# Two more pairs of the up-projection through Strassen's scheme, their mixed inputs summed on ScalarE and VectorE

## The chip, the cores and the metric

The kernel runs on one core of a Trainium2 chip. The metric is the device time of one launch in microseconds. Before the change three timed runs gave 702.15, 702.4 and 703.0 us, with a median of 702.4 us. Engines are named as the profile names them: PE is TensorE, PEld its weight loads, DVE is VectorE, ACT is ScalarE, POOL is GpSimd, and SP is SyncE, which here only issues transfers.

## The reference

One decoder layer on 512 tokens with a width of 1024: a combined input projection, two causal attentions of 8 heads each (block-sparse and stick-breaking), gates, an output projection and a residual, then a gated convolution block. The change lies in that last block:

```python
h = rms_norm(x, g_ffn[layer])
u = causal_depthwise_conv(h @ w_up[layer], conv_w[layer], conv_b[layer])   # h: 512 x 1024, w_up: 1024 x 5632
u_gate, u_val = jnp.split(u, 2, axis=-1)                                   # 2816 columns each
x = x + (jax.nn.silu(u_gate) * u_val) @ w_down[layer]
```

Everything is float32.

## The kernel before

**Three products for one.** A float32 operand is split into a high and a low part, each in the type that TensorE multiplies: ACT copies the high part (`hi`, `whi`), DVE subtracts it from the original to get the low part (`lo`, `wlo`). `mm3` (lines 90 to 92) then issues three matmuls: high by high, high by low, low by high.

**Pairs.** The up-projection is cut into 22 pairs. Pair i is a tile of 128 gate columns and the matching tile of 128 value columns; its contraction over 1024 runs in eight blocks of 128. `h2` holds the normalized input, transposed and split, for all eight blocks. A plain pair (`plain`, `up_mm`) is 2 columns tiles x 8 blocks x 3 = 48 matmuls that stream 512 tokens each. Its weights are two tiles of 128x1024, each split on the way by ACT (line 85) and DVE (line 86). The first two pairs are done in eight halves of 256 tokens (`up_half`), since the second half of the tokens is ready earlier; their weight tiles are the four entries of `wup`.

**Mixed pairs.** Pairs 4 to 19 (`MIXED`) go through the Winograd form of Strassen's scheme. Gate and value, the two halves of the tokens and the two halves of the contraction make a 2x2 by 2x2 block product, which takes seven block products of 256 tokens: 7 x 4 blocks x 3 = 84 matmuls. `first_four(i)` issues four of the seven, called X, Q, Y and Z here after the quarters of PSUM that they fill, `last_three(i)` the other three; the loop issues `first_four` of the next pair before `last_three` of the last one. X and Q use plain rows of `h2`; Y and Z of `first_four` and the first and last of `last_three` use four sums of quarters of the input, held split in `tm4` (tiles `xa7` to `xa10`).

**Weights of a mixed pair.** Four tiles: `wa` straight from the weights, `wb` and `wc` sums of weight quarters, `wd` a half tile straight from the weights. The sums (`usum`) are made in DRAM by accumulating transfers on POOL's queue, 16 pairs one after another, while the attention runs. The low part of `wc` is made ahead, too: during the gate stage `split_ahead` fetches the sum (`praw`), ACT writes its high part into a spare PSUM tile (line 604), DVE subtracts, and POOL stores the result (`ulo`); `last_three` later fetches it from there by SP straight into the `wlo` slot (line 991). ACT (line 992) and DVE (line 994) split everything else. High and low parts stand in rings of three slots each (`wsp`), so a weight tile can be written when the matmuls of the one three places before it have finished.

**Mixed inputs.** `h32` (tiles `xa5`, `xa6`) is the input in float32: 16 transfers on POOL's queue copy the high parts and accumulate the low parts (lines 1031 and 1033) behind pairs 0 and 1, while PE works on plain pairs 2 and 3. `mixes` makes the four sums on DVE and splits each (lines 965 to 971).

**Order.** PE runs in program order, by hand. The other engines' orders come from a scheduler; each engine takes its queue in order. Behind the products of a pair stand, on ACT and DVE, the sums of its seven parts (lines 1007 to 1024) and `glu` (lines 911 to 928, then 576 to 579 and 337/338): convolution, gate, and the sums for the down-projection. These free the PSUM banks: eight banks, two per pair.

## Time and profile before

| what | value |
| --- | --- |
| median of three timed runs | 702.4 us (702.15 to 703.0) |
| the profiled execution's own time | 701.36 us |
| its span | 699.6 us |
| PE busy | 690.9 us (99%), 4460 matmuls seen |
| PEld busy | 604.3 us (86%) |
| DVE busy | 573.7 us (82%) |
| ACT busy | 404.3 us (58%) |
| POOL busy | 123.8 us (18%) |
| plain pairs 2 and 3 on PE | 391.20 to 412.98 us |
| mixed pairs 4 to 19 on PE | 412.98 to 565.31 us |

Times inside the span are microseconds from its start. A row of the timeline gives the start, the duration, the engine, the line, the operation, output and inputs, the shape and the count; in brackets stands how long the engine had been idle before it and what ended that. The profile's page gives matmuls a duration of 0.28 or 0.39 us, but they overlap in a pipeline: what a matmul costs is the distance from one start to the next.

### The profile page before, as it was taken

The page shows a single profiled execution, that of the slowest core. Times are in us where ns is not written, and L with a number is a line of the kernel's source. Part 1 is how long each engine was busy: PE and PEld are TensorE (multiplying, and loading weights), DVE is VectorE, ACT ScalarE, POOL GpSimd, SP SyncE. Part 2 cuts the span into 40 slices and gives each one's busy share as a digit, 9 for nine tenths or more (in the row PEclk, how much of TensorE's full clock was granted, in tenths as well). Part 3 has the DMA queues.
Part 4 walks back from the last instruction along what each step waited for, and adds up shares of the span by engine and source line. Part 5 has one row for each costly group of instructions (what it writes and reads, how often), then busy time and mean ns, then how long its engine had stood idle before and what let it go on. Part 6 is the DMA issues. An engine that isn't in the chain of part 4 may idle for free.

```text
span 699.6 us, 11729 instructions
## 1 busy us (share of the span) xinstructions
PE 690.9 (99%) x4460; PEld 604.3 (86%) x4460; DVE 573.7 (82%) x901; ACT 404.3 (58%) x607; POOL 123.8 (18%) x200
## 2 busy tenths in 40 slices
PE   9999999999999999999999999999999999999995
PEld 6888888979888888888889889999999988888884
DVE  7778858598694777586876899989999998878996
ACT  6435445455564455445576666777777764546854
POOL 1211122233542122112312410000000003200000
PEclk9999999999999999999999999999999999999999
DMA  8799999999999688787998968889777765867703
GB/s 313 277 339 368 358 353 238 240 237 246 228 266 291 230 294 273 270 270 273 350 340 290 208 176 300 291 306 326 250 240 250 261 220 199 311 209 249 265 0 121
DMA packets 57577, 184.13 MB, mean 263 GB/s; under 512 B 6640, under 2 KB 7408, under 8 KB 51632
## 3 DMA queue, kind: packets, MB, share of 16 engines
q1 hardware_dynamic: 41136, 105.18, 42.5%
q0 software_dynamic: 16096, 77.87, 39.8%
q8 instruction: 35, 0.57, 0.3%
q10 hardware_dynamic: 288, 0.33, 0.1%
q14 instruction: 22, 0.18, 0.1%
HBM read 162.64 MB, written 64.75 MB: 325 GB/s over the span
## 4 chain that ended last, share of the span: by engine, by line
PE 98%; DVE 1%; ACT 1%; DMA 1%; issue 0%; ACTq 0%
PE b L92 12%; PE b L90 12%; PE b L91 12%; PE mm L90 11%; PE mm L92 11%; PE mm L91 11%; PE c L91 5%; PE c L90 5%; PE c L92 5%; PE q L209 3%; PE tp L480 3%; PE tp L504 3%; PE sc L404 1%; PE sc L414 1%; PE v L91 1%; PE v L90 1%
## 5 line engine op out<-in xcount | busy, mean ns | idle before, releaser
L90 PE MATMUL b<-h,whi 128*128 128x256 f32 (+1 forms) x320 | 95.8, 299 | 0.0
L91 PE MATMUL b<-h,whi 128*128 128x256 f32 (+1 forms) x320 | 95.7, 299 | 0.0
L92 PE MATMUL b<-h,wlo 128*128 128x256 f32 (+1 forms) x320 | 95.7, 299 | 0.0
L90 PE MATMUL mm<-xg,whi 128*128 128x512 f32 x224 | 89.8, 401 | 0.0
L85 ACT ACTIVATE whi<-raw 128x1024 fp32r<-128x1024 f32 (+2 forms) x62 | 59.8, 975 | 51.4 <-PE mm L92 16.8
L92 PE MATMUL mm<-xg,wlo 128*128 128x512 f32 x224 | 87.4, 390 | 0.0
L91 PE MATMUL mm<-xg,whi 128*128 128x512 f32 x224 | 87.3, 390 | 0.0
L992 ACT ACTIVATE whi<-raw 128x1024 fp32r<-128x1024 f32 x64 | 61.1, 954 | 37.5 <-PE b L91 28.1
L86 DVE TENSOR_TENSOR wlo<-raw,whi 128x1024 fp32r<-128x1024 f32 (+2 forms) x62 | 68.6, 1115 | 12.9 <-ACT whi L85 12.6
L90 PE MATMUL b<-xa,whi 128*128 128x256 f32 x256 | 70.7, 276 | 0.0
L91 PE MATMUL b<-xa,whi 128*128 128x256 f32 x256 | 70.7, 276 | 0.0
L672 ACT ACTIVATE whi<-raw 128x1024 fp32r<-128x1024 f32 x45 | 46.8, 1052 | 31.9 <-DVE raw L690 11.8
L90 PEld LDWEIGHTS b<-h,whi 128*128 128x128 f32 x320 | 60.1, 188 | 2.5
L91 PEld LDWEIGHTS b<-h,whi 128*128 128x128 f32 x320 | 60.1, 188 | 2.5
L92 PEld LDWEIGHTS b<-h,wlo 128*128 128x128 f32 x320 | 60.1, 188 | 2.5
L672 DVE TENSOR_TENSOR wlo<-raw,whi 128x1024 fp32r<-128x1024 f32 x45 | 54.7, 1221 | 5.7 <-ACT whi L672 5.6
L92 PE MATMUL b<-xa,wlo 128*128 128x256 f32 x192 | 53.0, 276 | 0.0
L90 PEld LDWEIGHTS mm<-xg,whi 128*128 128x128 f32 x224 | 42.1, 188 | 9.9 <-issue 1.8
L92 PEld LDWEIGHTS mm<-xg,wlo 128*128 128x128 f32 x224 | 42.0, 188 | 9.0
L91 PEld LDWEIGHTS mm<-xg,whi 128*128 128x128 f32 x224 | 42.2, 188 | 7.9
L91 PEld LDWEIGHTS b<-xa,whi 128*128 128x128 f32 x256 | 48.1, 188 | 0.0
L90 PEld LDWEIGHTS b<-xa,whi 128*128 128x128 f32 x256 | 48.1, 188 | 0.0
(282 smaller groups left out, 1747.4 us busy)
## 6 DMA issues: line engine op xcount, KB each, us to landing
raw<-w SPq DMA_DIRECT2D x103, 512.0 KB, 5.8
usum<-w POOLq DMA_DIRECT2D x16, 1024.0 KB, 25.6
raw<-usum SPq DMA_DIRECT2D x32, 512.0 KB, 5.2
usum<-w POOLq DMA_DIRECT2D x16, 512.0 KB, 19.6
usum<-usum POOLq DMA_DIRECT2D x32, 256.0 KB, 12.0
praw<-usum POOLq DMA_DIRECT2D x16, 512.0 KB, 5.6
ulo<-praw POOLq DMA_DIRECT2D x16, 512.0 KB, 5.3
wlo<-ulo SPq DMA_DIRECT2D x32, 256.0 KB, 3.6
```

Source lines behind the costliest of these rows:

```text
L85: wload.hi = nc.scalar.activation(hi[:, sl], raw[:, sl], AF.Copy)
L86: wload.lo = nc.vector.tensor_sub(lo[:, sl], raw[:, sl], hi[:, sl].bitcast(F32))
L90: nc.tensor.matmul(ps, a[0], b[0], start=start, stop=False, **kw)
L91: nc.tensor.matmul(ps, a[0], b[1], start=False, stop=False, **kw)
L92: nc.tensor.matmul(ps, a[1], b[0], start=False, stop=stop, **kw)
L209: nc.tensor.matmul(qk0[c], w0[i][:, (k % 2) * 512 + c * 128:(k % 2) * 512 + (c + 1) * 128], xg[k][:, j], start=(k == 0 and n == 0), stop=( ...
L404: nc.tensor.matmul(scs[h // 2][:, h % 2, o:o + n], Q[i][r0:r0 + 32, c, qt * 128:(qt + 1) * 128], K[i][r0:r0 + 32, d, :n], start=False, sto ...
L414: nc.tensor.matmul(sc[:, h, o:o + n], q[r0:r0 + 64, c, qt * 128:(qt + 1) * 128], k[r0:r0 + 64, d, :n], start=m == 0, stop=m == 2, skip_gro ...
L480: nc.tensor.transpose(tp[:, h, c:c + 128], a[:, h, c:c + 128], ident)
L504: nc.tensor.matmul(av[h * 64:(h + 1) * 64, j, qt * 128:(qt + 1) * 128], v[:, kb, (2 * p + h) * 64:(2 * p + h + 1) * 64], aT[p][:, h, o + k ...
L672: splits.append((nc.scalar.activation(hi, raw, AF.Copy), nc.vector.tensor_sub(lo, raw, hi.bitcast(F32))))
L992: nc.scalar.activation(hi[:, :n], raw[:, :n], AF.Copy)
```

## The change

Pairs 2 and 3 become mixed pairs (`MIXED = range(2, 20)`), so the mixed inputs are wanted right behind the first two pairs, where before two plain pairs stood in between.

- The 16 transfers that made `h32` are gone. ACT reads the first half of the tokens once more from the transposed PSUM banks (line 1054 of the new file, eight instructions of 128x256); DVE adds the high and low parts of the second half (line 1056, two of 128x1024). `mixes` needs one operation per sum as before, in another order, and hands out the four split inputs one by one; the splits of weights of the first mixed pair are put behind them (`early`, `ready`) by a new helper `behind`, which only puts instructions later in their engine's order.
- The last of the `up_half` calls run in the order 2, 0, 1, 3.
- POOL's queue makes the weight sums of 17 pairs (2 to 18) ahead; those of pair 19 are made later, in four steps behind pairs 8, 10, 12 and 14.
- `split_ahead` makes 16 low parts as before, but others: those of `wc` for pairs 2 to 15 and those of `wb` for pairs 2 and 3. Those of `wc` for pairs 16 to 19 are now split in the loop, by DVE.
- The small steps for the down-projection's sums behind pairs 0 to 2 are tied to another tile, and two small copies swap places at the end.

```diff
-MIXED = range(4, 20)
+MIXED = range(2, 20)
-AHEAD = MIXED
+AHEAD = sorted([(i, 1) for i in MIXED[:14]] + [(i, 0) for i in MIXED[:2]], key=lambda q: (q[0], -q[1]))
...
-        sums_of(MIXED)
+        for _ in sums_of(MIXED[:17]):
+            pass
+    lastsums = sums_of(MIXED[17:])
...
-    ulo = {i: wdr.tile([128, 2, 512], F32R, name=f"ulo{i}") for i in AHEAD}
+    ulo = {(i, h): wdr.tile([128, 2, 512], F32R, name=f"ulo{i}{h}") for i, h in AHEAD}
...
-        i = ahead.pop(0)
+        q = i, h = ahead.pop(0)
         raw = psp.tile([128, 2, 512], F32, name="praw", bufs=3)
-        nc.gpsimd.dma_start(raw, both(usum[i][2:4]))
+        nc.gpsimd.dma_start(raw, both(usum[i][2 * h:2 * h + 2]))
...
-    h2 = [x1s.tile([128, 2, S], F32R, name=f"h2{k}") for k in range(KT)]
+    h2all = x1s.tile([128, KT, 2, S], F32R, name="h2")
+    h2 = [h2all[:, k] for k in range(KT)]
...
-    for n in range(4):
+    for n in (2, 0, 1, 3):
         up_half(ups[n], wup[n], 0)
...
-        nc.vector.tensor_sub(b11, b11, b12)
-        nc.vector.tensor_sub(b12, b22, b12)
-        nc.vector.scalar_tensor_tensor(b22, b11, -1.0, b22, op0=OP.mult, op1=OP.subtract)
-        nc.vector.scalar_tensor_tensor(b21, b22, -1.0, b21, op0=OP.mult, op1=OP.subtract)
-        for n, q in enumerate((b11, b22, b12, b21)):
-            nc.scalar.activation(tm4[n][:, 0], q, AF.Copy)
-            nc.vector.tensor_sub(tm4[n][:, 1], q, tm4[n][:, 0].bitcast(F32))
+        def halve(n, q, sign=1.0):
+            hi, lo = tm4[n][:, 0], tm4[n][:, 1]
+            act = nc.scalar.activation(hi, q, AF.Copy, scale=sign)
+            return act.ins, nc.vector.scalar_tensor_tensor(lo, q, sign, hi.bitcast(F32), op0=OP.mult, op1=OP.subtract).ins
+        nc.vector.tensor_sub(b22, b22, b12)
+        yield halve(2, b22)
+        nc.vector.tensor_sub(b12, b11, b12)
+        yield halve(0, b12)
+        nc.vector.tensor_add(b11, b11, b22)
+        yield halve(1, b11, -1.0)
+        nc.vector.tensor_sub(b21, b11, b21)
+        yield halve(3, b21)
...
     def first_four(i):
-        wa = wmix(i, [(slice(0, 1024), w[WIDX["up", i, 0]])])
-        wb = wmix(i, [(None, both(usum[i][0:2]))])
+        with behind(early if i == MIXED[0] else ()):
+            wa = wmix(i, [(slice(0, 1024), w[WIDX["up", i, 0]])])
+            wb = wmix(i, [(None, both(usum[i][0:2]))], lo=ulo.get((i, 0)))
...
     def last_three(i, ps1, ps2, p1s, v):
-        wc = wmix(i, [(None, both(usum[i][2:4]))], lo=ulo.get(i))
+        wc = wmix(i, [(None, both(usum[i][2:4]))], lo=ulo.get((i, 1)))
...
+        if i in range(8, 16, 2):
+            step(lastsums, u[:, 0, :1])
...
-    for i in range(2):
-        plain(i)
-    for k in range(KT):
-        nc.gpsimd.dma_start(h32[k // 4][:, k % 4], h2[k][:, 0].bitcast(F32))
-    for k in range(KT):
-        nc.gpsimd.dma_start(h32[k // 4][:, k % 4], h2[k][:, 1].bitcast(F32), accum_op=OP.add)
-    for i in range(2, MIXED[0]):
-        if i == MIXED[0] - 1:
-            mixes()
-        plain(i)
+    for k in (0, 2, 1, 3, 4, 6, 5, 7):
+        src = turn_banks[0, k // 4][k % 4 // 2][:, k % 2 * 256:(k % 2 + 1) * 256]
+        nc.scalar.activation(h32[k // 4][:, k % 4, :256], src, AF.Copy, scale=gffn[:, k:k + 1])
+    for h in range(2):
+        nc.vector.tensor_add(quad(h, 1), *(h2all[:, 4 * h:4 * h + 4, c, 256:].bitcast(F32) for c in range(2)))
+    mixed_in = mixes()
+    early = next(mixed_in)
+    ready = next(mixed_in)
+    for i in range(MIXED[0]):
+        with behind(next(mixed_in, ())):
+            plain(i)
```

The rows of the program's order that follow name an instruction's line, operation, output and inputs with their buffer numbers, and shape.

**First place: DVE between the transposed input and the first product behind the `up_half` calls.** Before, the eight low parts of `h2` (line 808) are followed by the splits of two plain weight tiles and the convolutions of pairs 0 and 1:

```order
L808 SCALAR_TENSOR_TENSOR h25_3393<-b2_3379,vecs_85,h25_3393 128x256
L808 SCALAR_TENSOR_TENSOR h27_3395<-b3_3380,vecs_85,h27_3395 128x256
L86 TENSOR_TENSOR wlo_4170<-raw_4168,whi_4169 128x1024
L86 TENSOR_TENSOR wlo_4201<-raw_4199,whi_4200 128x1024
L912 SCALAR_TENSOR_TENSOR t0_4119<-b6_3850,vecs_85,t0_4119 128x511
L912 SCALAR_TENSOR_TENSOR t1_4123<-b7_3851,vecs_85,t1_4123 128x511
```

Now the input's float32 sums, the mixes and their low parts stand there, and the split of `wa` of pair 2 (`wlo_4176`) among them:

```order
L815 SCALAR_TENSOR_TENSOR h2_3394<-b3_3386,vecs_85,h2_3394 128x256
L1056 TENSOR_TENSOR xa5_4107<-h2_3394 128x4x256
L1056 TENSOR_TENSOR xa6_4108<-h2_3394 128x4x256
L978 TENSOR_TENSOR xa6_4108<-xa6_4108,xa5_4107 128x4x256
L980 TENSOR_TENSOR xa5_4107<-xa5_4107 128x4x256
L976 SCALAR_TENSOR_TENSOR xa9_4111<-xa6_4108,xa9_4111 128x1024
L982 TENSOR_TENSOR xa5_4107<-xa5_4107,xa6_4108 128x4x256
L1008 TENSOR_TENSOR wlo_4176<-raw_4174,whi_4175 128x1024
L976 SCALAR_TENSOR_TENSOR xa7_4109<-xa5_4107,xa7_4109 128x1024
L984 TENSOR_TENSOR xa6_4108<-xa5_4107,xa6_4108 128x4x256
L976 SCALAR_TENSOR_TENSOR xa8_4110<-xa5_4107,xa8_4110 128x1024
L919 SCALAR_TENSOR_TENSOR t0_4138<-b6_3849,vecs_85,t0_4138 128x511
```

The convolutions of pairs 0 and 1 have moved behind the third of the four mixed inputs.

**Second place: SP's queue there.** Before, only raw weights and sums are loaded until the first `wc`. Now the low parts of `wb` of pairs 2 and 3 (`ulo20`, `ulo30`) and of `wc` of pair 2 (`ulo21`) stand between the loads:

```order
L1002 DMA raw_4306<-usum2_433 128x2x512
L1005 DMA wlo_4182<-ulo20_2627 128x512 x2
L1002 DMA raw_4313<-w 128x512
L1002 DMA raw_4373<-w 128x1024
L1005 DMA wlo_4248<-ulo30_2629 128x512 x2
L1005 DMA wlo_4308<-ulo21_2626 128x512 x2
L1002 DMA raw_4379<-usum4_435 128x2x512
```

Each of the three writes a `wlo` slot and so stands in the queue until the matmuls on the slot's last tile are done.

**Third place: DVE around the last mixed pairs.** Before, between the products of pair 18 and those of pair 19 (`wlo_6261` and `wlo_6267` are `wa` and `wb` of pair 19, `whi_6332` is the half tile `wd` of pair 18; `wc` comes from DRAM):

```order
L338 TENSOR_TENSOR xa1_5986<-tm_5857,xa1_5986 128x1024
L994 TENSOR_TENSOR wlo_6261<-raw_6259,whi_6260 128x1024
L1009 TENSOR_TENSOR xb8_4095<-b1_6137,xb8_4095 128x256
L1022 TENSOR_TENSOR u_6238<-b4_6006,xb9_4096 128x256
L1023 TENSOR_TENSOR u_6238<-b4_6006,xb9_4096 128x256
L928 TENSOR_TENSOR tm_6121<-t0_6112,t1_6116 128x2x256
L994 TENSOR_TENSOR wlo_6267<-raw_6265,whi_6266 128x1024
L1024 TENSOR_TENSOR u_6238<-b5_6007,xb10_4097 128x512
L577 TENSOR_TENSOR tm_6121<-tm_6121 128x256
L994 TENSOR_TENSOR whi_6332<-raw_6331,whi_6332 128x512
```

Now (`wlo_6378` and `wlo_6384` are `wa` and `wb` of pair 19, `wlo_6443` is `wc` of pair 18):

```order
L1008 TENSOR_TENSOR wlo_6378<-raw_6376,whi_6377 128x1024
L585 TENSOR_TENSOR xb7_4093<-tm_5976,xb7_4093 128x256
L1031 TENSOR_TENSOR xb8_4094<-b1_6255,xb8_4094 128x256
L921 SCALAR_TENSOR_TENSOR t1_6234<-u_6226,vecs_85,t1_6234 128x510
L344 TENSOR_TENSOR xa1_6105<-tm_5976,xa1_6105 128x1024
L1008 TENSOR_TENSOR wlo_6384<-raw_6382,whi_6383 128x1024
L1044 TENSOR_TENSOR u_6355<-b4_6125,xb9_4095 128x256
L1045 TENSOR_TENSOR u_6355<-b4_6125,xb9_4095 128x256
L1046 TENSOR_TENSOR u_6355<-b5_6126,xb10_4096 128x512
L1008 TENSOR_TENSOR wlo_6443<-raw_6441,whi_6442 128x1024
L937 TENSOR_TENSOR tm_6239<-t0_6230,t1_6234 128x2x256
L1008 TENSOR_TENSOR whi_6448<-raw_6447,whi_6448 128x512
```

The split of `wc` is new there, and the sums, the convolution and the gate product of earlier pairs have moved behind the splits of weights.

More of the change, by code (lines that the diff above doesn't have):

```diff
@@ L279, in sums_of @@
                     nc.gpsimd.dma_start(usum[i], flat(("ui", i, 0), 2), max_dma_last_dim=8192)
+                yield
                 for i in group:
                     adds(usum[i][0:2], flat(("ui", i, 2), 1))
+                yield
                 for i in group:
                     adds(usum[i][3], usum[i][0])
+                yield
                 for i in group:
                     adds(usum[i][2], usum[i][3])
-        sums_of(MIXED)
+                yield
+        for _ in sums_of(MIXED[:17]):
+            pass
+    lastsums = sums_of(MIXED[17:])
     mqkp = pool(ysta, "mqkp", 4, side="right")
@@ L595, in both, with step @@
         return q.rearrange("h p c -> p h c")
+    dsums = (step for q in dsum.items() for step in quarter_sums("di", [q]))
+    marks = iter(list(range(16, 31)) + list(range(16)))
+    def step(todo, src):
+        c = next(marks, None)
+        if c is None:
+            return
+        seen = small[:, c:c + 1]
+        nc.vector.tensor_copy(seen, src)
+        with tc.issue_after(nc.gpsimd.tensor_copy(seen, seen).ins):
+            next(todo, None)
     def split_ahead():
@@ L607, in split_ahead @@
             nc.vector.tensor_sub(lo, raw, phi.bitcast(F32))
-        nc.gpsimd.dma_start(ulo[i], lo)
+        nc.gpsimd.dma_start(ulo[q], lo)
     for i in range(KT):
@@ L656, in trunk_layer @@
     splits = []
-    dsums = (step for q in dsum.items() for step in quarter_sums("di", [q]))
-    marks = iter(list(range(16, 31)) + list(range(8)))
-    def step(todo, src):
-        c = next(marks, None)
-        if c is None:
-            return
-        seen = small[:, c:c + 1]
-        nc.vector.tensor_copy(seen, src)
-        with tc.issue_after(nc.gpsimd.tensor_copy(seen, seen).ins):
-            next(todo, None)
     def split_in(p, raw):
@@ L927, in glu @@
         j = i // 2
+        if i < 3:
+            step(dsums, uc[0][:, :1])
         split = a_side(i % 2, lambda dst: nc.vector.tensor_mul(dst, ua, ub), glu.tm, xa[j] if i % 2 else None, xb[j])
@@ L939, in glu @@
                     nc.gpsimd.dma_start(away["a", j][:, h], xa[j][:, h])
-        if i < 3:
-            step(dsums, xb[j][:, 0, :1] if i % 2 else glu.tm[:, 0, :1])
         return split
@@ L995, in wmix, with behind @@
         return hi, wlo
+    def behind(ins):
+        st = ExitStack()
+        for q in ins:
+            st.enter_context(tc.issue_after(q))
+        return st
     def first_four(i):
-        wa = wmix(i, [(slice(0, 1024), w[WIDX["up", i, 0]])])
-        wb = wmix(i, [(None, both(usum[i][0:2]))])
+        with behind(early if i == MIXED[0] else ()):
+            wa = wmix(i, [(slice(0, 1024), w[WIDX["up", i, 0]])])
+            wb = wmix(i, [(None, both(usum[i][0:2]))], lo=ulo.get((i, 0)))
         ps1, ps2 = up_ps(), up_ps()
@@ L1006, in first_four @@
         p1s, p5s, v = (tmp[i % 2][:, n] for n in range(3))
-        nc.scalar.activation(p1s, X, AF.Copy)
+        with behind(ready if i == MIXED[0] else ()):
+            nc.scalar.activation(p1s, X, AF.Copy)
         nc.scalar.activation(p5s, Y, AF.Copy)
@@ L1025, in last_three @@
                              ps2.rearrange("p (n c) -> p n c", n=2), u2[:, None].to_broadcast([128, 2, 256]))
+        if i in range(8, 16, 2):
+            step(lastsums, u[:, 0, :1])
         return glu(i, (u[:, 0], u[:, 1]))
-    for i in range(2):
-        plain(i)
-    for k in range(KT):
-        nc.gpsimd.dma_start(h32[k // 4][:, k % 4], h2[k][:, 0].bitcast(F32))
-    for k in range(KT):
-        nc.gpsimd.dma_start(h32[k // 4][:, k % 4], h2[k][:, 1].bitcast(F32), accum_op=OP.add)
-    for i in range(2, MIXED[0]):
-        if i == MIXED[0] - 1:
-            mixes()
-        plain(i)
+    for k in (0, 2, 1, 3, 4, 6, 5, 7):
[9 more added lines that the diff above has]
+            plain(i)
     prev = None
     for i in MIXED:
-        cur = i, *first_four(i)
+        with behind(ready if i == MIXED[0] + 1 else ()):
+            cur = i, *first_four(i)
         if prev:
```

## The prediction

> **What bounds the kernel now.** I read the page first: engines, slices, the chain that ended last.
>
> ```profile
> span 699.6 us, 11729 instructions
> PE 690.9 (99%) x4460; PEld 604.3 (86%) x4460; DVE 573.7 (82%) x901; ACT 404.3 (58%) x607; POOL 123.8 (18%) x200
> PE   9999999999999999999999999999999999999995
> DVE  7778858598694777586876899989999998878996
> PE 98%; DVE 1%; ACT 1%; DMA 1%; issue 0%; ACTq 0%
> ```
>
> PE is busy in every slice but the last and makes up 98% of the chain: matmul time taken away shortens the run one for one, unless PE then waits. DVE is the next engine, at nine tenths and more where the mixed pairs run, so it is where a wait would come from. Then PE's starts at three edges, and the windows between them:
>
> ```profile
> 391.20 0.40 PE L90 MATMUL b<-h,whi 128*128 128x512 f32 x1
> 412.98 0.28 PE L90 MATMUL b<-h,whi 128*128 128x256 f32 x1
> 565.31 0.40 PE L90 MATMUL b<-h,whi 128*128 128x512 f32 x1
> 391.20:412.98 21.78, 21.78 (x98) 18.02 (x97) 19.58 (x30) 12.91 (x15) 6.75 (x10) 1.00 0.93 209
> 412.98:565.31 152.33, 152.33 (x1345) 152.32 (x1344) 144.94 (x226) 112.30 (x169) 4.39 (x8) 1.00 0.79 272
> ```
>
> A window's columns are its length, then the busy time of PE, PEld, DVE, ACT and POOL, the granted clock, the share of DMA and GB/s. Plain pairs 2 and 3 take 21.78 us, the sixteen mixed pairs 152.33 us; PE has no gap in either, at full clock.
>
> **What goes and what comes on PE.** Two plain pairs are 96 matmuls of 512: 21.78 / 96 = 0.227 us each. Sixteen mixed pairs are 16 x 84 = 1344 of 256: 152.33 / 1344 = 0.1133 us, half as much, so a mixed pair costs 152.33 / 16 = 9.52 us. Two of them take 19.04 us, and PE gains 21.78 - 19.04 = **2.74 us**.
>
> The half price has to hold for the added 168 matmuls. The Trainium skill, TensorE: Matmul & The Clock Gate, section Back-to-back issue gap, speaks against it: weight loads and matmuls together set a sustained spacing of about 81 ns at N=128 and 131 ns at N=512. On a straight line through the two a 256-wide matmul would take 98 ns, an estimate from that page, and the change would cost 168 x 98 - 96 x 131 ns = 3.9 us. This trace does not agree: 227 ns and 113 ns. The worst 256-wide spacing in the trace is that of one `up_half`:
>
> ```profile
> 385.60 0.28 PE L90 MATMUL b<-h,whi 128*128 128x256 f32 x1
> 385.72 0.28 PE L91 MATMUL b<-h,whi 128*128 128x256 f32 x1
> ```
>
> At 0.12 us the gain would be 21.78 - 168 x 0.12 = 1.62 us. I take 0.1133, the mean of the 1344 matmuls of the very form that is added.
>
> **The gap in front of pair 2.** The order of PE up to 391.20 keeps its count, so X of pair 2 starts there; by 12 matmuls a quarter (1.36 us), Q starts at 392.6, Y at 393.9, Z at 395.3, pair 3 at 396.6, `last_three(2)` at 402.1 and its last quarter at 404.8. What has to be ready:
>
> ```profile
> 379.08 0.86 ACT L807 ACTIVATE h<-b,vecs 128x256 fp32r<-128x256 f32 x2 [0.21 <-DVE h L808]
> 382.96 1.06 ACT L85 ACTIVATE whi<-raw 128x1024 fp32r<-128x1024 f32 x1 [3.02 <-PE b L91]
> 385.68 1.06 ACT L85 ACTIVATE whi<-raw 128x1024 fp32r<-128x1024 f32 x1 [1.66 <-PE b L91]
> 379.58 0.88 DVE L808 SCALAR_TENSOR_TENSOR h<-b,vecs,h 128x256 fp32r<-128x256 f32 x2 [0.15 <-ACT h L807]
> 410.82 1.22 DVE L966 TENSOR_TENSOR xa<-xa,xa 128x1024 f32<-128x1024 f32 x1
> 411.95 0.74 DVE L914 SCALAR_TENSOR_TENSOR t<-b,vecs,t 128x510 f32<-128x510 f32 x1
> 380.46:384.06 3.60, 3.60 (x34) 3.60 (x33) 0.01 (x2) 1.06 (x1) 2.50 (x4) 1.00 1.01 390
> ```
>
> `h2` is done at 379.94 on ACT and 380.46 on DVE, and behind it DVE stood idle for 3.6 us. A DVE operation of 128x1024 takes 1.13 us to the next start (410.82 to 411.95), an ACT read of 128x256 0.42 (half of 0.86), an ACT split 1.06. No row shows line 1056's sum of strided parts; it moves as much as L966 and is taken as that, 1.13, with 2 x 1.13 as the upper bound. The scale and sign of the other forms change no shape.
>
> ACT: eight reads, 379.94 + 8 x 0.42 = 383.3. DVE: two sums to 382.7, first mix to 383.9, second to 385.1. ACT splits `xa9` from 384.0 to 385.1. The `wsp` slots come free when the second, third and fourth of the last four `up_half` end (2.7 us apart; 382.96 and 385.68 are ACT waiting for the first two): 385.7, 388.4, 391.2. So ACT does the high part of `wa` 385.7 to 386.8, `xa7` to 387.8, `wb` 388.4 to 389.5, `xa8` to 390.5. DVE: low part of `xa9` to 386.3, third mix to 387.5, `wa` to 388.6, `xa7` to 389.8, fourth mix to 390.9, `xa8` to 392.1, two convolution steps, `wa` of pair 3 to 394.5, `xa10` to 395.7. Against 391.4, when PE first needs a low part of `wa`, that leaves 2.8 us; `xa7` has 4.1 us to Y, `wa` of pair 3 2.1 us, the others more. The upper bound on line 1056 adds 2.3 us and still fits, if barely. So I cost it at **nothing**; without that cover each microsecond late would be one on PE. The sixteen transfers it replaces were covered by plain pairs, so they give nothing back.
>
> Three low parts now come by SP: those of `wb` for pairs 2 and 3 and of `wc` for pair 2. Each waits in SP's queue for its slot (388.4, 393.9, 396.6), and the loads of `wd` and of the next pairs wait behind it; those are wanted over 9 us later. The second piece is issued some 0.5 us after the slot is free and wanted at 394.1, 399.6 and 402.3, so 5.2 us are left for its landing.
>
> ```profile
> wlo<-ulo SPq DMA_DIRECT2D x32, 256.0 KB, 3.6
> wlo<-ulo SPq DMA_DIRECT2D x2, 256.0 KB, 5.3
> DMA to landing us min/median/max: 2.5/3.8/10.0
> ```
>
> The median is 3.6, that of the slowest couple (454 to 460 us) 5.3; the last line also holds the stores of `ulo`. So **nothing** to 3 x 0.1 us, and 3 x 4.8 = 14.4 us if all three landed at 10.0.
>
> **POOL's queue.** One more pair's sums stand in front of `praw`:
>
> ```profile
> 212.76 0.76 POOL L246 DMA_DIRECT2D usum<-usum  x1 [1.03 <-DMA usum<-usum]
> 214.22 0.77 POOL L602 DMA_DIRECT2D praw<-usum  x1 [0.70 <-DVE g L536]
> 70.35 0.52 POOL L279 DMA_DIRECT2D usum<-w  x1 [3.11 <-issue]
> 74.03 0.52 POOL L279 DMA_DIRECT2D usum<-w  x1 [3.17 <-issue]
> praw<-usum POOLq DMA_DIRECT2D x3, 512.0 KB, 12.2
> 233.30 1.03 ACT L604 ACTIVATE spare<-praw 128x1024 fp32r<-128x1024 f32 x1 [1.29 <-DVE praw L607]
> 234.87 1.06 ACT L85 ACTIVATE whi<-raw 128x1024 fp32r<-128x1024 f32 x1 [0.54 <-PE mm L91]
> ```
>
> A copy takes 3.7 us of the queue and three adds at most as much each, so the first `praw` is issued at about 224 (at the latest 229) and the second, 2.4 us later, lands about 238 by the 12.2 us of that stretch. ACT's split of it, now at 233.30, then comes 5 us later, and with it the next weight's high part, now at 234.87. Its slot has only just come free, and two weight tiles of 24 x 0.227 = 5.4 us each are used before it: PE needs it at 245. **Nothing**; 5 us beyond would decide.
>
> **DVE at the end.** Pairs 16 to 19 get one split of 1.13 us more each, ahead in DVE's queue of the sums and convolutions. DVE works 144.94 / 16 = 9.06 us per pair; with it 10.19, where PE gives 9.52: it falls back 0.67 us a pair, 2.7 us in all.
>
> ```profile
> 531.16 1.22 DVE L994 TENSOR_TENSOR wlo<-raw,whi 128x1024 fp32r<-128x1024 f32 x1
> 533.89 1.22 DVE L994 TENSOR_TENSOR wlo<-raw,whi 128x1024 fp32r<-128x1024 f32 x1
> 532.90 0.28 PE L92 MATMUL b<-h,wlo 128*128 128x256 f32 x1
> 565.31:592.00 26.69, 26.69 (x119) 21.78 (x117) 24.71 (x39) 15.30 (x19) 4.43 (x7) 1.00 0.55 184
> ```
>
> Even now the low part of `wa` of pair 17 is done at 532.38 for a matmul at 532.90. But the new order pushes the late work behind the splits, and that late work frees banks of which there are four pairs' worth. Going through the new queue with these starts (1.13 for a split, 0.66 for a convolution step, 0.34 for a sum of 256), each split ends in time, the tightest being `wb` of pair 19, 0.3 to 0.5 us ahead. The backlog of 2.7 us is worked off in the plain pairs, where DVE has 2.0 us free, and later. I take **0.2 us** of waiting; bounds 0 and 2.7, and 4.5 if DVE's present waits stayed as well.
>
> **Sum.** 2.74 - 0.2 is about 2.5: the profiled execution of 701.36 us (span 699.6) becomes 698.8. It lies 1.04 us under the median of 702.4, which becomes **699.8 us**.
>
> **The rivals.** (1) *DVE becomes the bound of pairs 16 to 19.* For it: 95% busy, margins of half a microsecond. Against: the new order, the four pairs of banks. If the backlog reaches PE whole, 2.74 - 2.7: 702.4. If the waits before convolutions (9.52 a pair with them) stay on top of the splits, 4 x 1.13 = 4.5 is lost: 702.4 + 1.8 = **704.2, slower**. It decides once a split ends over 0.5 us later than worked out. (2) *The low parts land late.* Over 6.1 us a piece at all three places eats the gain; 8 us gives 702.4 - 2.74 + 3 x 2.8 = 708. Against: under 5.4 everywhere in the loop, and the sixteen transfers around them are gone. (3) *`praw` late, ACT stuck, PE waits.* The latest issue, 229, leaves about nothing of the cover; 2 us lost is 701.7. (4) *The mixes don't fit the gap.* 3 us late: 702.7. (5) *Narrow matmuls cost more than half.* 0.12 us each: 700.8. By the page named above it would be 706.3.
>
> **How the numbers follow.** Forecast 0.60; (1) 0.18, of it 0.06 slower; (2) 0.07; (3) 0.06; (4) 0.05; (5) 0.04. A measurement of this kernel tells about 0.2%, 1.4 us, from no change. Faster, below 701.0: the forecast, (5), and somewhat over half of (1) to (3) where the loss stays partial, 0.76. Same 0.14, slower 0.10. The forecast's own range is 699.2 to 700.6 (0 to 0.8 us of waiting, spread of runs); the one for 8 in 10 reaches into partial losses of (1) and (3): 698.9 to 702.0.
>
> **What would show it.** Right: the distance from the first matmul of pair 2 to the first of plain pair 20 is 18 x 9.52 = 171.4 us without idle PE, and pair 20 starts at about 562.6. Wrong: idle PE at 391 to 405 released by DVE, ACT or a transfer; idle PE between 520 and 563 released by DVE's splits; idle PE between 225 and 260. A mixed spacing over 0.1133 us would show (5).

## The result, and the profile after

The change makes the kernel slower. Its median is 706.46 us over 14 runs (703.84 to 710.91), beside 702.14 us over 14 runs of the kernel before (701.43 to 703.1): a ratio of 1.006, with a 95% interval of 1.0043 to 1.0077. (A ratio here stands on all runs of both kernels, so it can differ a little from that of the two medians.) The runs also spread over 7 us, where those of before spread over 1.7. The profiled execution took 709.48 us, in the upper part of that spread; its span is 707.8 us, 8.2 us more than before.

The page of the changed kernel: span, engines, and the chain that ended last.

```profile
span 707.8 us, 11909 instructions
PE 693.6 (98%) x4532; PEld 608.2 (86%) x4532; DVE 582.2 (82%) x923; ACT 411.8 (58%) x625; POOL 124.6 (18%) x200
PE 58%; DMA 18%; issue 17%; POOL 4%; DVE 2%; ACT 1%; SPq 0%; POOLq 0%; DVEq 0%; ACTq 0%
```

The chain was PE alone (98%) before. Now it also runs through transfers and POOL, so something other than PE set the time. The view of PE's waits says where; its columns are the time in all, the number of waits and the longest.

```profile
PE c L91 <- DVE wlo L679: 2.4, 1, 2.4
PE mm L90 <- ACT whi L85: 1.5, 1, 1.5
PE mm L159 <- DVE warmb L153: 1.3, 1, 1.3
PE mm L92 <- DVE wlo L86: 0.7, 1, 0.7
PE b L92 <- DMA wlo<-ulo: 0.6, 2, 0.5
```

The wait of 1.3 us at the start was there before; the others are new, and come to 5.2 us. That is less than the loss, so I laid PE's starts at the edges of the stages side by side: first the kernel before, then the changed one.

```profile
225.20 0.50 PE L90 MATMUL mm<-xg,whi 128*128 128x512 f32 x1
365.72 0.48 PE L90 MATMUL b<-whi,xs 128*128 128x512 f32 x1
587.10 0.39 PE L90 MATMUL c<-whi,xa 128*128 128x512 f32 x1
```

```profile
226.11 0.50 PE L90 MATMUL mm<-xg,whi 128*128 128x512 f32 x1
370.98 0.48 PE L90 MATMUL b<-whi,xs 128*128 128x512 f32 x1
569.01 0.40 PE L90 MATMUL b<-h,whi 128*128 128x512 f32 x1
590.80 0.39 PE L90 MATMUL c<-whi,xa 128*128 128x512 f32 x1
```

| stretch | before, us | after, us | difference |
| --- | --- | --- | --- |
| up to the gate stage | 225.20 | 226.11 | +0.91 |
| gate stage and output projection | 140.52 | 144.87 | +4.35 |
| `up_half`, plain and mixed pairs, up to plain pair 20 | 199.59 | 198.03 | -1.56 |
| plain pairs 20 and 21 | 21.79 | 21.79 | 0 |
| down-projection, first pass (its second begins at 647.36 and 655.21) | 60.26 | 64.41 | +4.15 |
| the rest, to the end of the span | 52.3 | 52.6 | +0.3 |

The forecast gain of 2.74 us is in the third row, less 1.18 us. Three places took it back: the gate stage, a low part among the mixed pairs, and the down-projection. The 0.91 us at the start is spread and not the change's: in the fourteen traces of this case that first row lies anywhere between 225.16 and 226.11 us, and in a second trace of the changed kernel it is at 225.44.

**The gate stage.** Timelines of before (ACT, then PE) and after (POOL, ACT and PE), at one weight of the gates:

```profile
268.31 1.03 ACT L604 ACTIVATE spare<-praw 128x1024 fp32r<-128x1024 f32 x1 [5.17 <-DMA praw<-usum]
271.93 1.04 ACT L85 ACTIVATE whi<-raw 128x1024 fp32r<-128x1024 f32 x1
278.37 0.39 PE L90 MATMUL mm<-xg,whi 128*128 128x512 f32 x1
```

```profile
226.55 0.77 POOL L620 DMA_DIRECT2D praw<-usum  x1 [1.31 <-DMA usum<-usum]
276.18 1.03 ACT L622 ACTIVATE spare<-praw 128x1024 fp32r<-128x1024 f32 x1 [6.80 <-DMA praw<-usum]
279.80 1.04 ACT L85 ACTIVATE whi<-raw 128x1024 fp32r<-128x1024 f32 x1
280.89 0.50 PE L90 MATMUL mm<-xg,whi 128*128 128x512 f32 x1 [1.45 <-ACT whi L85]
282.35 0.50 PE L92 MATMUL mm<-xg,wlo 128*128 128x512 f32 x1 [0.72 <-DVE wlo L86]
284.10 0.63 PE L91 MATMUL mm<-xg,whi 128*128 128x512 f32 x1
284.52 0.63 PE L92 MATMUL mm<-xg,wlo 128*128 128x512 f32 x1
```

The first `praw` is issued 12.3 us later than before (214.22). Fifty microseconds on, the `praw` that ACT waits for is still 7.9 us behind. The weight split stands behind it in ACT's queue and ends at 280.84, where PE wanted it at 279.28: 1.6 us. Before, the same split ended at 272.97 for a matmul at 278.37, with 5.4 us in hand. Of the 4.35 us that the stage loses, 1.6 are this wait and 0.9 the next one, for the low part of the same weight. The last two rows show where the rest went: matmuls start 0.43 us apart, where 0.227 is usual. The window view of the stretch, with the granted clock (1.00 is full speed) as third column from the right:

```profile
282.35:286.60 4.25, 4.25 (x12) 3.33 (x13) 4.25 (x5) 3.62 (x5) 1.29 (x2) 0.60 0.69 171
```

PE counts as busy there, so no view of waits shows this part.

**The low part.** From the timelines of POOL and PE, and the transfers of 476 to 480 us:

```profile
471.46 0.53 POOL L279 DMA_DIRECT2D usum<-w  x1
wlo<-ulo SPq DMA_DIRECT2D x2, 256.0 KB, 8.1
484.34 0.39 PE L92 MATMUL b<-xa,wlo 128*128 128x256 f32 x1 [0.46 <-DMA wlo<-ulo]
```

The first step of pair 19's late sums (1 MB) is issued here and takes 8.8 us. The low part of `wc` of pair 10 is issued at 476.88, beside it and beside three stores of finished pairs, and takes 8.1 us (the middle of its two halves) where the other fifteen low parts take 3.0 to 5.1.

**The down-projection.** The chain of waits of the changed kernel there:

```profile
598.53 1.14 DVE raw L697
599.70 7.97 DMA raw<-w
607.76 1.23 DVE raw L697
608.99 1.15 DVE wlo L679
610.18 0.50 PE c L91
```

L697 sums two raw weights of the down-projection; its end frees the slot into which the next raw weight is loaded, whose sum and split PE waits for.

### The profile page after: what moved, and what is told of

Same layout as the page of the kernel before. It is cut to its first block, busy times and chain, and to the rows that moved or that the text cites. A ratio compares the mean times of both kernels' runs of the same rounds, so it can differ in the third digit from the quotient of the medians.

```text
span 707.8 us, 11909 instructions
## 1 busy us (share of the span) xinstructions
PE 693.6 (98%) x4532; PEld 608.2 (86%) x4532; DVE 582.2 (82%) x923; ACT 411.8 (58%) x625; POOL 124.6 (18%) x200
## 4 chain that ended last, share of the span: by engine, by line
PE 58%; DMA 18%; issue 17%; POOL 4%; DVE 2%; ACT 1%; SPq 0%; POOLq 0%; DVEq 0%; ACTq 0%
PE b L92 12%; PE b L90 12%; PE b L91 12%; DMA usum<-usum 7%; PE c L91 4%; PE c L92 4%; PE c L90 4%; PE q L209 3%; DMA usum<-w 3%; DMA osum<-osum 2%; PE mm L92 2%; PE mm L91 2%; PE mm L90 2%; DMA ulo<-praw 2%; DMA raw<-w 2%
## 5 line engine op out<-in xcount | busy, mean ns | idle before, releaser
L1006 ACT ACTIVATE whi<-raw 128x1024 fp32r<-128x1024 f32 x72 | 68.7, 954 | 44.6 <-PE b L91 33.7
L92 PE MATMUL b<-h,wlo 128*128 128x256 f32 (+1 forms) x312 | 90.0, 288 | 0.2 <-DMA wlo<-ulo 0.2
L90 PE MATMUL b<-h,whi 128*128 128x256 f32 (+1 forms) x312 | 90.0, 288 | 0.0
L91 PE MATMUL b<-h,whi 128*128 128x256 f32 (+1 forms) x312 | 89.9, 288 | 0.0
L90 PE MATMUL b<-xa,whi 128*128 128x256 f32 x288 | 79.5, 276 | 0.0
L91 PE MATMUL b<-xa,whi 128*128 128x256 f32 x288 | 79.5, 276 | 0.0
L85 ACT ACTIVATE whi<-raw 128x1024 fp32r<-128x1024 f32 (+2 forms) x58 | 55.5, 968 | 37.6 <-PE mm L92 16.8
L86 DVE TENSOR_TENSOR wlo<-raw,whi 128x1024 fp32r<-128x1024 f32 (+2 forms) x58 | 63.7, 1111 | 5.9 <-ACT whi L85 5.6
L679 ACT ACTIVATE whi<-raw 128x1024 fp32r<-128x1024 f32 x45 | 47.0, 1052 | 35.4 <-DVE raw L697 10.0
L92 PE MATMUL b<-xa,wlo 128*128 128x256 f32 x216 | 59.7, 277 | 0.5 <-DMA wlo<-ulo 0.5
L91 PEld LDWEIGHTS b<-xa,whi 128*128 128x128 f32 x288 | 54.1, 188 | 0.0
L90 PEld LDWEIGHTS b<-xa,whi 128*128 128x128 f32 x288 | 54.1, 188 | 0.0
L612 POOL COPY small<-small 128x1 f32<-128x1 f32 x31 | 19.8, 720 | 189.8 <-DVE small L611 189.5
L90 PEld LDWEIGHTS mm<-xg,whi 128*128 128x128 f32 x224 | 42.5, 190 | 11.9 <-ACT whi L85 1.9
```

The costliest lines, as they stand in the source:

```text
L85: wload.hi = nc.scalar.activation(hi[:, sl], raw[:, sl], AF.Copy)
L86: wload.lo = nc.vector.tensor_sub(lo[:, sl], raw[:, sl], hi[:, sl].bitcast(F32))
L90: nc.tensor.matmul(ps, a[0], b[0], start=start, stop=False, **kw)
L91: nc.tensor.matmul(ps, a[0], b[1], start=False, stop=False, **kw)
L92: nc.tensor.matmul(ps, a[1], b[0], start=False, stop=stop, **kw)
L612: with tc.issue_after(nc.gpsimd.tensor_copy(seen, seen).ins):
```

## The experiments

What I held after reading the two traces: (A) the 17th pair's sums delay `praw`, which stalls the gate stage; (B) the late sums of pair 19 slow the low parts; (C) DVE's four late splits push its work into the down-projection. Rivals: transfers that vary by chance, and the mixed inputs in the gap. In all kernels the lines that are not shown are those of the changed kernel, unless stated; the diffs are shortened.

### The gap alone

```diff
-MIXED = range(2, 20)
+MIXED = range(2, 18)
...
-        for _ in sums_of(MIXED[:17]):
+        for _ in sums_of(MIXED):
...
-        if i in range(8, 16, 2):
-            step(lastsums, u[:, 0, :1])
```

> Edit: sixteen pairs are mixed, 2 to 17; pairs 18 and 19 are plain. The sums of sixteen pairs are made ahead, none late; DVE splits the wc of pairs 16 and 17 in the loop. So the work on PE is that of the kernel before, and the gap in front of pair 2 is that of the changed kernel. Theory (the mixed inputs fit the gap and cost nothing; what was lost came from the 17th and 18th pair's sums and from DVE's four late splits): no PE wait between 380 and 420 us and none in the gate stage; the median lies within 1.5 us of the kernel before, 702 to 703.5, the rest being DVE's two late splits. Rival (the early mixed inputs themselves cost time): PE waits between 390 and 410 us, or a median above 704 with no wait in the gate stage.

702.72 us against 701.91, a ratio of 1.0006 (0.9997 to 1.0015). PE's only wait beside the one at the start:

```profile
PE c L91 <- DVE small L611: 0.6, 1, 0.6
```

Nothing in the gate stage, nothing between 380 and 420 us, and the stretch up to the first plain pair behind the mixed ones takes 177.79 us: 199.59 less the two plain pairs' 21.78, to 0.02 us. Moving the mixed inputs in front of the first mixed pair costs nothing; the loss lies in what the 17th and 18th pair bring.

### Sums ahead: one pair fewer, one pair more

One kernel makes the sums of sixteen pairs ahead, and those of 18 and 19 late:

```diff
-        for _ in sums_of(MIXED[:17]):
+        for _ in sums_of(MIXED[:16]):
...
-    lastsums = sums_of(MIXED[17:])
+    lastsums = sums_of(MIXED[16:])
```

> Edit: POOL makes the weight sums of 16 pairs ahead of the attention's end, as many as before the change; those of pairs 18 and 19 both come late, in the same four steps behind pairs 8, 10, 12 and 14, each step twice as large. Theory (the first praw is late because a 17th pair's sums stand ahead of it, and ACT's queue then stands still in front of a gate weight): the first praw is issued at about 215 us, the PE wait at 279 to 282 us and the slow matmuls behind it are gone, 4.4 us less; the waits for low parts around pair 10 to 12 grow from 1.2 us, since the late sums beside them move twice the bytes; the wait in the down stage stays. Median about 703. Rival (transfers in the gate stage vary from run to run, and the wait there has nothing to do with the 17th pair): PE still waits between 270 and 290 us, and the median stays at 706 or above.

The other makes all eighteen ahead:

```diff
-        for _ in sums_of(MIXED[:17]):
+        for _ in sums_of(MIXED):
...
-        if i in range(8, 16, 2):
-            step(lastsums, u[:, 0, :1])
```

> Edit: POOL makes the sums of all 18 mixed pairs ahead of praw, none late. Theory: another 12 us of POOL's queue ahead of the first praw (about 238 us), so the wait in the gate stage grows, by up to those 12 us; no PE wait for a low part in the mixed pairs, since the transfers that slowed it are gone; the wait in the down stage stays. Median 708 to 716. Rival (the waits in the gate stage are chance): that stage as in the changed kernel, and the median falls by about 1 us to 705. Rival on the low part (its transfer is slow whatever runs beside it): PE still waits 0.5 us or more for a low part at some mixed pair.

The first took 711.29 us (ratio 1.0129, 1.0105 to 1.0153), the second 711.57 us (1.0135, 1.0104 to 1.0166). Both are slower than the changed kernel, for opposite reasons; the second as expected (708 to 716). From the timelines of the first (POOL, PE):

```profile
214.97 0.77 POOL L620 DMA_DIRECT2D praw<-usum  x1 [0.66 <-DMA usum<-usum]
492.53 0.58 PE L92 MATMUL b<-xa,wlo 128*128 128x256 f32 x1 [2.73 <-DMA wlo<-ulo]
```

and of the second:

```profile
234.42 0.78 POOL L620 DMA_DIRECT2D praw<-usum  x1 [0.78 <-DMA usum<-usum]
249.48 0.79 PE L90 MATMUL mm<-xg,whi 128*128 128x512 f32 x1 [3.00 <-ACT whi L85]
```

With the first `praw` at 215, 227 and 234 us the gate stage and output projection take 140.51, 144.87 and 152.42 us. Over all traces of this case: in the eight with sixteen or fewer low parts and the first `praw` ahead of 215.6 us it is 140.5 each time, in the five with the first `praw` between 224.6 and 234.4 it is 141.1 to 152.4, the later the longer. So (A) holds, and chance alone does not; but how late `praw` is varies between executions of one kernel, and the loss with it (0.6 us with 224.61 and 4.35 with 226.55, both in the changed kernel). The low part the other way round: without late sums the stretch from 378.20 us up to plain pair 20 takes 196.84 us, just what 199.59 - 2.74 asks for, and PE waits for no low part; with one pair late it loses 1.2 us, with two 6.2 us (the low parts of `wc` of pairs 10 and 11, and slow matmuls behind the wait of 2.73). The low part of pair 10 takes 5.4 us without late sums, 8.1 beside a step of 1 MB and 8.6 beside one of 2 MB. (B) holds too. The expectation for the first kernel was wrong in its total, 703: I had let the loss grow from 1.2 us without saying by how much, and it outweighed the cure. Its traced execution, 707.51 us, is the fastest of its six, so no trace shows what the median loses beyond that.

### Late sums in small pieces

```diff
-    lastsums = sums_of(MIXED[17:])
+    lastsums = fine_sums(MIXED[-1])     # 4 copies of a quarter, 2 adds from w, 2 adds within usum; a yield behind each
...
-        if i in range(8, 16, 2):
+        if i in range(6, 14):
```

> Edit: the late sums of pair 19 are cut into eight transfers of 256 KB, one behind each of the pairs 6 to 13, in place of four steps of up to 1 MB behind pairs 8, 10, 12 and 14. The same bytes move. Theory (what makes the low parts of pairs 10 to 12 late is that a whole step's bytes move at once with the transfers of the pair that is stored away): no PE wait over 0.3 us between 396 and 569 us; the waits in the gate stage and in the down stage stay as in the changed kernel; median 704 to 706, some 1 us below the changed kernel. Rival (any bytes on that queue make them late): waits of the same size, 1.2 us in sum, at more places.

702.56 us against 702.03, a ratio of 1.0008 (0.9994 to 1.0021): better than expected (704 to 706). Its edges of the third stretch:

```profile
367.08 0.48 PE L90 MATMUL b<-whi,xs 128*128 128x512 f32 x1
563.91 0.40 PE L90 MATMUL b<-h,whi 128*128 128x512 f32 x1
```

That is 196.83 us: the gain of 2.74 us, whole. The same bytes cost nothing when they move 256 KB at a time; the low part of pair 10 takes 6.4 us. That the median fell by some 4 us is more than the 1.2 us that (B) took in the trace of the changed kernel, and why is not settled: in this profile the gate stage, with its first `praw` at 224.64 us, lost only 0.9 us and the first pass of the down-projection only 0.45, though neither was cured.

### The changed kernel once more

> The changed kernel once more, unaltered, for a second trace. Theory: waits at the same three places (a gate weight around 280 us, a low part of pair 10 to 12, the second sum of down weights), each of another size; matmul spacing doubled for 3 to 4 us behind each wait of over 1.5 us and not behind shorter ones. Rival (chance): waits at other places.

One execution of 704.30 us. Its waits:

```profile
PE c L91 <- DVE wlo L679: 2.1, 1, 2.1
PE b L92 <- DMA wlo<-ulo: 0.3, 1, 0.3
PE mm L92 <- DVE wlo L86: 0.3, 1, 0.3
```

The same three places, of other sizes: 0.6 us in the gate stage and output projection, 0.7 in the mixed pairs, 3.8 in the down-projection. The places are the change's; how much each takes differs between executions of the same kernel, most likely with how long the transfers in the chain happen to take. That fits the spread of 7 us.

### DVE's late splits

In the changed kernel, spread out:

```diff
-AHEAD = sorted([(i, 1) for i in MIXED[:14]] + [(i, 0) for i in MIXED[:2]], key=lambda q: (q[0], -q[1]))
+AHEAD = sorted([(i, 1) for i in MIXED if i not in (4, 9, 14, 19)] + [(i, 0) for i in MIXED[:2]], key=lambda q: (q[0], -q[1]))
```

> Edit: the same sixteen low parts are made ahead in number, but those that DVE splits in the loop are the wc of pairs 4, 9, 14 and 19 in place of 16 to 19. Theory (DVE's backlog of the last four pairs reaches the down stage through the first sums of down weights there): DVE works the single splits off between them, the wait of 2.4 us and the slow matmuls behind it in the down stage are gone, some 4 us less; the gate stage and the late low part stay as in the changed kernel. Median 702 to 703.5. Rival (a weight's transfer is late in the down stage and DVE has no part in it): PE waits there as before, median about 706.

And alone, in the kernel before:

```diff
-AHEAD = MIXED
+AHEAD = MIXED[:12]
```

> Edit: the kernel before, with one part of the change alone: low parts are made ahead for the wc of pairs 4 to 15 only, and DVE splits the wc of pairs 16 to 19 in the loop. Theory (four late splits are enough to push DVE's work into the down stage): PE waits 0.8 to 2.5 us around the second sum of down weights, with slow matmuls behind a wait of over 1.5 us; the first sum there starts about 7.6 us behind the first down matmul in place of 6.5; no wait in the mixed pairs; median 703 to 706. Rival (DVE works the splits off in the plain pairs and the wait came from slow transfers): within 0.7 us of the kernel before, 701.3 to 702.7. Second rival (the splits bind at once): PE waits between 520 and 565 us.

Spread out, the median is 704.66 us (ratio 1.003, 1.0015 to 1.0045), above the 702 to 703.5 that were expected, and the first pass of the down-projection takes 60.79 us in place of 64.41. Alone, it is 702.41 us against 701.72, a ratio of 1.0009 (1.0000 to 1.0018): below the expected 703 to 706, and as the first rival had it by the total, though the sum in the next rows comes as late as the theory said. The first two sums of down weights in that kernel, and PE's wait:

```profile
595.41 1.22 DVE L690 TENSOR_TENSOR raw<-raw 128x1024 f32<-128x1024 f32 x1
603.08 1.23 DVE L690 TENSOR_TENSOR raw<-raw 128x1024 f32<-128x1024 f32 x1 [1.10 <-DMA raw<-w]
PE c L91 <- DVE wlo L672: 0.7, 1, 0.7
```

Its first down matmul is at 587.77, so the first sum comes 7.64 us behind it. In the kernel before it was 6.52 (593.62 - 587.10), in the changed kernel 7.65, spread out 6.62. So four late splits do put DVE 1.1 us behind there, and that becomes a wait of 0.7 us. The changed kernel's 2.4 us has a second part: the load between the two sums took 7.97 us there, 7.63 us in the repeat and 6.39 us here. What slows it, I did not settle; the transfers that bring stored pairs back run beside it in all of them. (C) holds for part of the loss, not for all.

### Cures together

Sixteen pairs' sums ahead, two pairs late in pieces of 256 KB behind pairs 2 to 15. In one kernel the late pairs are 18 and 19 and DVE's splits stay at 16 to 19:

```diff
+LATE = (18, 19)
...
-        for _ in sums_of(MIXED[:17]):
+        for _ in sums_of([i for i in MIXED if i not in LATE]):
...
-    lastsums = sums_of(MIXED[17:])
+    lastsums = late_sums()     # fine_sums of both, the second six pairs behind the first
...
-        if i in range(8, 16, 2):
+        if i in range(2, 16):
```

> Edit: the changed kernel with two of the three cures: sums of sixteen pairs ahead, those of pairs 18 and 19 late in eight transfers of 256 KB each, behind pairs 2 to 15; DVE splits the wc of pairs 16 to 19 as in the changed kernel. Theory: no wait in the gate stage, none over 0.3 us in the mixed pairs, the wait in the down stage as in the changed kernel, 1 to 4 us with the slow matmuls; median 700.5 to 703. Rival (the down stage's wait was due to the larger late sums): below 700.5.

In a second one DVE's splits are spread as well:

```diff
-LATE = (18, 19)
+LATE = (14, 18)
-AHEAD = sorted([(i, 1) for i in MIXED[:14]] + [(i, 0) for i in MIXED[:2]], key=lambda q: (q[0], -q[1]))
+AHEAD = sorted([(i, 1) for i in MIXED if i not in (6, 10, *LATE)] + [(i, 0) for i in MIXED[:2]], key=lambda q: (q[0], -q[1]))
```

> Edit: the changed kernel with all three causes taken away. Sums of sixteen pairs ahead, those of pairs 14 and 18 late, in eight transfers of 256 KB each, one or two behind each of the pairs 2 to 15; DVE splits the wc of pairs 6, 10, 14 and 18 in place of 16 to 19. Theory (the three places explain the loss): first praw at about 215 us and no wait in the gate stage; no wait over 0.3 us in the mixed pairs; at most 0.8 us in the down stage; the gain of 2.74 us on PE comes out, a median of 699.3 to 700.8. Rival (DMA has no room for two pairs' late sums however they are cut): waits for low parts of 1 us or more between 400 and 530 us, median 702 or above.

A third, made from the second, mixes seventeen pairs:

```diff
-MIXED = range(2, 20)
+MIXED = range(2, 19)
-LATE = (14, 18)
+LATE = (14,)
...
-        if i in range(2, 16):
+        if i in range(3, 11):
```

> Edit: as the kernel with the three cures, but seventeen pairs are mixed, 2 to 18, and only the sums of pair 14 are late, one piece behind each of the pairs 3 to 10; DVE splits the wc of pairs 6, 10 and 14; pair 19 is plain. Theory: half of the gain on PE, 1.37 us, and half of the late bytes: median 700.3 to 701.3, above the kernel with the three cures by 0.5 to 1.4 us. Rival (DMA has no room for late sums): below that kernel.

They took 701.99 us (ratio 1.0005, 0.9995 to 1.0015), 701.83 us (0.9997, 0.9985 to 1.0008) and 701.74 us (0.9998, 0.9989 to 1.0006). In all three the gate stage and output projection are back at 140.51 or 140.52 us, and no low part is late by 0.3 us. But none is faster than before. In the first, PE waits 0.9 us in the down-projection, with no slow matmuls behind it, and its first pass takes 61.27 us, 1.0 more than before. In the second, the expectation of 699.3 to 700.8 was too low. Its mixed pairs keep 1.78 us of the gain: behind each of the single splits at pairs 6, 10 and 14 two matmuls in a row start 0.21 to 0.23 us apart in place of 0.113, 0.6 us in all, and the rest is in smaller pieces. The down-projection's first pass loses 0.95 us, and in this execution the gate stage begins 0.74 us later than in that of before, which is the spread of the start. The third, with half of the gain to expect, was to lie 0.5 to 1.4 us above the second and does not; between kernels so close together the runs do not decide.

Two more tried to take DVE's splits away in another manner. Eighteen low parts made ahead, from the first of these kernels:

```diff
-AHEAD = sorted([(i, 1) for i in MIXED[:14]] + [(i, 0) for i in MIXED[:2]], key=lambda q: (q[0], -q[1]))
+AHEAD = sorted([(i, 1) for i in MIXED if i not in LATE] + [(i, 0) for i in MIXED[:2]], key=lambda q: (q[0], -q[1]))
```

> Edit: as the one before, and eighteen low parts are made ahead in place of sixteen: DVE splits only the wc of pairs 18 and 19 in the loop. Theory (half the backlog, and the chain of low parts starts 12 us earlier than in the changed kernel, so that two more fit): no wait in the gate stage, at most 0.8 us in the down stage; the gain of 2.74 us on PE comes out at last, median 699.3 to 700.8. Rival (two more low parts overfill the gate stage): PE waits between 270 and 325 us, median above 701.5.

707.0 us (ratio 1.0083, 1.0056 to 1.011): the rival. The last `praw` now comes at 317.9 us in place of 303.0, into the output projection, whose first weights stand behind it on ACT and DVE:

```profile
PE b L91 <- DVE small L634: 2.5, 1, 2.5
```

And POOL, which subtracts nothing else there, in place of DVE for the `wc` of 16 to 19, also from the first of these kernels:

```diff
-            nc.vector.tensor_sub(wlo, raw[:, :n], hi[:, :n].bitcast(F32))
+            by.tensor_sub(wlo, raw[:, :n], hi[:, :n].bitcast(F32))     # by = nc.gpsimd for wc, nc.vector for the rest
```

> Edit: as the kernel with two cures (sums of pairs 18 and 19 late in pieces of 256 KB, four late wc), but POOL in place of DVE splits the wc of pairs 16 to 19 in the loop; POOL has no other work there. Theory (DVE's four late splits push its work 1.1 us into the down stage): the first sum of down weights starts about 6.5 us behind the first down matmul in place of 7.6, PE waits at most 0.3 us there, and the gain on PE comes out: median 699.3 to 701.0. Rival (POOL is too slow for it, or DVE slows beside it): PE waits for those low parts between 530 and 565 us, or DVE's operations of 128x1024 take longer than 1.23 us there; median 701.5 or above.

705.98 us (ratio 1.0051, 1.0038 to 1.0065): the rival again. Timelines of POOL and DVE, and PE's wait:

```profile
542.59 2.38 POOL L1031 TENSOR_TENSOR wlo<-raw,whi 128x1024 fp32r<-128x1024 f32 x1 [4.89 <-ACT whi L1029]
542.84 3.21 DVE L1031 TENSOR_TENSOR wlo<-raw,whi 128x1024 fp32r<-128x1024 f32 x1
PE b L93 <- DVE wlo L1031: 3.4, 3, 1.6
```

DVE's own split, begun while POOL subtracts, takes 3.21 us in place of 1.22; the six of them between 528 and 563 us average 1.86 us (four keep 1.22), and PE waits for low parts, 3.4 us in all. The stretch with the mixed pairs takes 203.01 us, 6.2 more than 196.84. The other half of the theory is borne out: without DVE's late splits the first pass of the down-projection is back at 60.39 us.

## Why the prediction was wrong

It gave 699.8 us, 698.9 to 702.0, and 0.10 for slower. Its central mechanism is there, and the failures lie in what it costed at nothing or too low. In the traced execution the gain of 2.74 us stands against 4.35 us in the gate stage, 1.18 at a low part and 4.15 in the down-projection; in the repeat, whose time is nearer the median, against 0.6, 0.7 and 3.8.

**Right: the gain on PE.** Narrow matmuls keep half the price, and the 2.74 us come out to within 0.02 where nothing is late (196.83 and 196.84 us in place of 199.59). The estimate of a loss of 3.9 us, made from the Trainium skill (TensorE: Matmul & The Clock Gate, section Back-to-back issue gap), does not hold here: the 1512 mixed matmuls of the changed kernel start 0.1133 us apart, its waits left out. That its total of 706.3 lies by the measured 706.46 is chance.

**Right: the gap.** The program there runs 5.26 us later than in the working. The low part of `wa` was put at 388.6, so 393.9; it is done at 393.99:

```profile
385.64 2.35 DVE L1056 TENSOR_TENSOR xa<-h 128x1024 f32<-128x1024 f32 x2
392.77 1.22 DVE L1008 TENSOR_TENSOR wlo<-raw,whi 128x1024 fp32r<-128x1024 f32 x1
```

The unseen sum of strided parts takes 1.18 us, not twice that. The second pieces of the three low parts at the start landed in 3.4 to 4.8 us, within the 5.2 us left for them, and nobody waited. PE waits for no DVE split in pairs 16 to 19, so rival (1), at 0.18, did not come true.

**Wrong: POOL's queue.** The working had the first `praw` at 224 us, at the latest 229, and it came at 226.55, which is right; the failed step is the sentence that follows, "PE needs it at 245. Nothing". It tested the weight behind the second `praw` and no other. There are sixteen `praw` through three buffers, each fetch waiting for the store of the one three places before it, so a late start is carried along. The weight that failed was another one, and the trace of before had it: 272.97 against 278.37, a cover of 5.4 us, less than the 7.9 us that were left of the delay of 12. Rival (3) was the right one for this place, at 0.06, with 2 us; it took 4.35 us in one profile and 0.6 in the other.

**Wrong: the late sums of pair 19 have no term.** The text has them in neither the sum nor a rival. Rival (2) looked for late low parts at the three new transfers, and took as evidence against it that sixteen transfers around them are gone; the part that came late was that of pair 10, beside a step of 1 MB that the change had put there. It cost 1.2 us, and with the step doubled two low parts cost 6.2.

**Wrong: "the backlog of 2.7 us is worked off in the plain pairs, where DVE has 2.0 us free, and later".** 1.1 us of it is still there at the first sum of down weights, which sets when the next raw weight is loaded. No late step was worked through behind the plain pairs. Alone it makes a wait of 0.7 us, with a load that is 1.6 us slower one of 2.4; why that load was slower stays open.

**Wrong: every wait was priced at its own length.** The wait of 1.6 us at 279 became 4.35 with the one for the low part and the matmuls at half speed behind them. The down-projection's 2.4 became 4.15. The working had no such term, and this is part of why its chance for slower was too small: a wait that fails its cover by little can cost far more than by how much it fails. It need not: gate-stage waits of 0.3 and 0.6 us, in the repeat and with the late sums in small pieces, were not followed by slow matmuls.

## What to carry to other kernels

Where a change delays the head of a chain that runs through a few buffers, test the delay against the cover of every consumer along the chain, not of the first. Transfers that a change moves into a stage have a price there even if nothing waits for them: cut them to pieces that end before the next transfer with a deadline begins. And in a kernel whose matrix engine never waits, a first long wait may be paid for twice: once as idle time, and once more in slow matmuls that count as busy.

## What the runs showed of the hardware

**Half speed behind a wait.** Behind waits of 2.06 us (the repeat), 2.38 (the changed kernel), 2.52 (eighteen low parts) and 2.73 (two pairs late), and behind pairs of waits of 1.03 + 0.72, 1.45 + 0.72, 1.54 + 0.71 and 3.00 + 0.79, the next 6 to 11 matmuls started at twice the usual distance, some 1.2 to 1.6 us more. But the length of a wait does not decide alone: behind one of 2.35 us (two pairs late, ended at 609.91) they did not. The granted clock tells more. In all fourteen traces it changes only at times that lie whole multiples of 3.413 us apart: each stretch at half speed between start and end of the program lasts one such step, once two, and the two in the changed kernel begin at 283.02 and 610.70 us, 96 steps apart. Windows on this grid, of the changed kernel and of the one with two pairs late:

```profile
279.61:283.02 3.41, 1.41 (x5) 0.89 (x6) 3.35 (x4) 3.41 (x5) 0.00 (x0) 1.00 0.83 285
283.02:286.44 3.42, 3.42 (x10) 2.63 (x9) 3.42 (x5) 2.95 (x4) 1.29 (x2) 0.50 0.77 189
```

```profile
604.72:608.13 3.41, 2.83 (x13) 2.02 (x11) 1.77 (x2) 0.00 (x0) 0.00 (x0) 1.00 0.68 214
608.13:611.54 3.41, 1.63 (x7) 1.37 (x8) 3.41 (x5) 2.79 (x4) 0.00 (x0) 1.00 0.69 197
611.54:614.96 3.42, 3.42 (x17) 2.84 (x16) 3.42 (x6) 0.69 (x1) 3.24 (x3) 1.00 0.59 195
```

In the first, PE is busy for 1.41 us of a step, so idle for 2.00, and the next step runs at half clock. In the second, an edge of the grid cuts the wait of 2.35 us into 0.58 and 1.78, and no step is slow. Over all fourteen traces, away from start and end, each of the seven steps in which PE was idle for 2.00 us or more was followed by one at half clock. Of those with less, two were: one of 1.75 us (late splits spread out) and one of 1.67 that was at half clock itself (all eighteen ahead). Two of 1.76 and 1.78 us were not, nor was any below 1.67. The grid lies differently in each execution, so the same wait can be paid for once or twice; that this is part of the spread of 7 us is likely, but no run tests it. The Trainium skill, TensorE: Matmul & The Clock Gate, section What's actually happening, tells of a clock that halves after an idle window of about 3.4 us and comes back after a busy one as long. The halving and the length of 3.41 us agree; here a window that was idle for 2.0 us of it brought it on all the same.

**POOL holds DVE up.** One subtraction of 128x1024 on POOL took 2.4 to 3.6 us, and a DVE operation beside it up to 2.0 us more than its 1.22. No run has POOL's subtraction with DVE idle, so whether DVE holds POOL up, too, is not shown. The Trainium skill, GPSIMD Engine Reference, section 1. Specifications, says that POOL's way into SBUF is shared with VectorE, with contention where VectorE's instruction has two inputs from there; these rows agree.

**One set of transfer engines.** A load on SP's queue of 256 KB took 8.1 us beside 1 MB and three stores on POOL's queue, 5.4 us beside the stores alone (the same load with all eighteen pairs' sums ahead), and the others of the changed kernel 3.0 to 5.1 us. The Trainium skill, DMA: Bandwidth & Descriptors, section Issuing engines are not separate DMA queues, says that transfers of all queues interleave on the same sixteen engines, which agrees.
